# An expert layer's second matrix split in full for the large experts, with the router's steps in another order

## The chip, the cores and the metric

The kernel runs on one NeuronCore of one Trainium2 chip. The metric is the device time of one execution in microseconds. An execution is also recorded by the hardware profiler, and all durations below come from that one record.

## The reference

One decoder layer over 1024 tokens of width 1024, in float32: a modulated RMSNorm, a projection to two groups of attention heads (one dilated, one differential), an output projection with a gated residual, and then the part that matters here, a second norm and a mixture of 32 experts, of which each token takes four:

```python
h2 = rms_norm(x, norm2_g) * (1.0 + scale2) + shift2
logits = h @ w_router + b_router
top_val, top_idx = lax.top_k(logits, TOP_K)          # 4 of 32
gates = jax.nn.softmax(top_val, axis=-1)
...
def expert_block(args):
    xe, e = args
    gu = xe @ w_gate_up[e] + b_gate_up[e]            # 1024 -> 2048
    g = jnp.minimum(gu[:, :D_FF], SWIGLU_LIMIT)
    u = jnp.clip(gu[:, D_FF:], -SWIGLU_LIMIT, SWIGLU_LIMIT)
    act = (u + 1.0) * (g * jax.nn.sigmoid(SWIGLU_ALPHA * g))
    return act @ w_down[e] + b_down[e]               # 1024 -> 1024
...
return x + gate2 * y                                 # y: gate-weighted sum over a token's experts
```

All weights are float32: 3 x 1024 x 1024 numbers, 12 MB per expert.

## The kernel before

Tokens lie in eight blocks of 128. After attention (to about 608 us) the **router stage** runs block by block (`Block`, the loop over `b`), then the **expert stage** (744 to 2139 us) takes the 32 experts one after the other. On TensorE, ScalarE, VectorE and SyncE the instructions run in the order in which the code is written; GpSimd's order is set by the scheduler.

**Router stage.** For a block, `turn` transposes the attention rows, `products(n, ks)` multiplies eight k-tiles of them by one half of the output matrix (three products per tile), and `add` (L885, L886) adds the residual and squares it. The loop works on three blocks at a time: products of block `b`; for `b-1` the second norm, the transposes of its residual rows (`turn_x1`, L901), `rows_out` (VectorE's L909, GpSimd's L910, then a store of the rows to `h2d`) and `logits` (products with the router, top four by L920 to L924); for `b-2` `places` (each token's place within its expert), `listed` (products L958 that make the list of the first expert's tokens) and `scattered` (VectorE's L971 to L977 work out slot numbers, then four indirect stores by GpSimd, L979, write token and gate into a table `tab`). `TA`, `TC` say after which of the eight k-tiles the steps of the other blocks come. After the last block VectorE sorts the experts by their number of tokens (`key`, `order`).

**Expert stage.** Experts are taken in an order fixed in sorted ranks, with room for a fixed number of tokens ("places") per rank, large and small in turn: 172, 136, 200, 128, 136, 128, 188, 128, 140, 124, ..., 144, 120, 168, 116, 144, ..., 156, 96, so 17 of the 32 have 136 places or more. "Place 16" below is the one with 144 places at 1465 to 1506 us, place 17 the 120 behind it. Rows are gathered from `h2d` by GpSimd (L1144, `stage_g`), transposed on TensorE (L1172, `stage_t`) and split there into a high part, a remainder and a bf16 copy.

A weight matrix comes in chunks of 512 x 512 (1 MB, 12 per expert, numbered 0 to 11). A **split** chunk goes in two halves: ScalarE copies the high part (L826, `hb`), VectorE subtracts it from the chunk and stores the remainder as bf16 (L813, `ha`). `products` multiplies by it: 32 instructions L1194 (high weights by high part and remainder of the rows, side by side) and 32 instructions L1200 (remainder weights by the bf16 rows) for a quarter of a matrix. A **plain** chunk (numbers 8 and 9, the first half of `w_down`) is not split: L1250 takes it from its buffer `draw` at full precision. `pump(upto)` issues chunk loads while a buffer is free (`NRING` = 6 for split chunks, `NPL` = 2 for plain ones) and splits as long as no more than `NH` = 12 halves are ahead. `done` is called at 14 events in each expert, and the table `TG` says how many halves may have been split by each of them (`NSP` = 20 per expert).

An expert runs through four `products` calls for gate and up columns. After each, ScalarE evacuates one part of the sums with the bias (L1214, `tb`) and VectorE joins it with the other (L1216, L1218), with sigmoid (L1226, L1227), clamp (L1235) and product (L1236), into `a`. Then the plain half: for each of its two chunks 32 products L1250, in whose middle `a` is split for later (ScalarE's copy L1254, VectorE's L1255, GpSimd's cast L1256), and behind which the next expert's rows are transposed (`between`). ScalarE evacuates the four sums of the plain half (L1262) into `yT`, a tile of the buffer `ay` that also holds `a`. Then the split half (`products` with `ax`, `ab`), its four evacuations L1270 on ScalarE and the joins L1271 on VectorE. The result is transposed back (L1279) one event later, scaled by the gate and added to the output by an indirect store (L1180).

## Time and profile before

| | us |
|---|---|
| three runs | 2153.43, 2152.49, 2149.2 |
| median | 2152.49 |
| the profiled execution | 2153.28 |
| its span | 2151.5 |
| attention and before | to about 608 |
| router stage, start of the experts | 608 to 744 |
| expert stage | 744 to 2139 |

Engines are named PE (TensorE products), PEld (its weight loads), DVE (VectorE), ACT (ScalarE), POOL (GpSimd) and SP (SyncE, which issues the weight loads); L1194 is line 1194 of the kernel. A profile row tells how long an engine worked; whether that matters is told by the chain of work that ended last and by what an engine waited for.

### The profile page before, as it was taken

The page shows a single profiled execution, that of the slowest core. Times are in us where ns is not written, and L with a number is a line of the kernel's source. Part 1 is how long each engine was busy: PE and PEld are TensorE (multiplying, and loading weights), DVE is VectorE, ACT ScalarE, POOL GpSimd, SP SyncE. Part 2 cuts the span into 40 slices and gives each one's busy share as a digit, 9 for nine tenths or more (in the row PEclk, how much of TensorE's full clock was granted, in tenths as well). Part 3 has the DMA queues.
Part 4 walks back from the last instruction along what each step waited for, and adds up shares of the span by engine and source line. Part 5 has one row for each costly group of instructions (what it writes and reads, how often), then busy time and mean ns, then how long its engine had stood idle before and what let it go on. Part 6 is the DMA issues. An engine that isn't in the chain of part 4 may idle for free.

```text
span 2151.5 us, 43844 instructions
## 1 busy us (share of the span) xinstructions
PE 2042.9 (95%) x16922; PEld 1913.2 (89%) x16922; DVE 1643.5 (76%) x2831; ACT 1355.7 (63%) x2391; POOL 503.5 (23%) x473
## 2 busy tenths in 40 slices
PE   6999999999899599999999999999999999999997
PEld 5877778998777599999999999999999999999997
DVE  6587765777666778788788878888788878878884
ACT  3522314777633377677677677676777777768774
POOL 2255532112045411112111121111111211221211
PEclk9999999999999799999999999999999999999998
DMA  8267786442324599799899999999999999999993
GB/s 294 67 167 221 216 240 166 112 106 71 107 99 147 181 329 306 255 331 342 273 295 353 288 316 312 333 308 323 320 309 310 358 309 325 326 328 327 325 324 99
DMA packets 273654, 549.53 MB, mean 255 GB/s; under 512 B 31795, under 2 KB 31811, under 8 KB 273315
## 3 DMA queue, kind: packets, MB, share of 16 engines
q1 hardware_dynamic: 251507, 490.61, 67.7%
q0 software_dynamic: 21936, 56.09, 11.2%
q8 instruction: 134, 2.20, 0.4%
q14 instruction: 77, 0.63, 0.1%
HBM read 501.84 MB, written 44.78 MB: 254 GB/s over the span
## 4 chain that ended last, share of the span: by engine, by line
PE 45%; DVE 13%; ACT 9%; issue 6%; DMA 2%; POOL 0%; SPq 0%; ACTq 0%; POOLq 0%; DVEq 0%
PE gu L1194 25%; PE gu L1200 11%; PE gu L1250 5%; DVE ha L813 5%; ACT hb L826 4%; PE gu L1279 2%; PE po L605 1%; ACT ay L1262 1%; DMA eraw<-in_w_gate_up_dram 1%; DMA eraw<-in_w_down_dram 1%; DVE ax L1255 1%; ACT tb L1214 1%; DVE su L1235 1%; DVE su L1216 1%; DVE ixf L924 1%
## 5 line engine op out<-in xcount | busy, mean ns | idle before, releaser
L813 DVE TENSOR_TENSOR ha<-eraw,hb 128x1024 bf16<-128x1024 f32 x640 | 762.8, 1245 | 1.6 <-ACT hb L826 1.6
L826 ACT ACTIVATE hb<-eraw 128x1024 fp32r<-128x1024 f32 x640 | 634.2, 1051 | 13.4 <-DMA eraw<-in_w_down_dram 11.1
L1194 PE MATMUL gu<-xx,hb 128*128 128x256 f32 (+13 forms) x4096 | 587.7, 300 | 3.6 <-DVE xx L1176 3.6
L1194 PEld LDWEIGHTS gu<-xx,hb 128*128 128x128 f32 x4096 | 554.2, 190 | 4.5 <-DVE xx L1176 4.3
L1200 PEld LDWEIGHTS <-ha 128*128 128x128 bf16 x5120 | 310.8, 97 | 11.9 <-issue 1.5
L1200 PE MATMUL gu<-xb,ha 128*128 128x128 bf16 (+19 forms) x4096 | 271.6, 224 | 0.0
L1250 PE MATMUL gu<-ay,draw 128*128 128x128 f32 (+19 forms) x2048 | 267.6, 289 | 1.7 <-DVE ay L1236 1.7
L1250 PEld LDWEIGHTS gu<-ay,draw 128*128 128x128 f32 x2048 | 257.3, 191 | 2.7 <-DVE ay L1236 2.1
L1214 ACT ACTIVATE tb<-gu,bcol 128x128 f32<-128x128 f32 (+19 forms) x512 | 157.7, 370 | 97.2 <-PE gu L1200 85.5
L1194 PE MATMUL gu<-ax,hb 128*128 128x256 f32 (+13 forms) x1024 | 159.1, 314 | 26.1 <-ACT ay L1262 25.7
L1180 POOL DMA_INDIRECT out_dram<-y,slot x47 | 81.1, 1726 | 404.6 <-ACT y L1280 258.2
L1194 PEld LDWEIGHTS gu<-ax,hb 128*128 128x128 f32 x1024 | 148.5, 203 | 30.0 <-ACT ay L1262 28.8
L1144 POOL DMA_INDIRECT xg<-h2d,slot x47 | 70.3, 1496 | 352.9 <-PE gu L1172 89.2
L571 DVE CUSTOM_DVE_ANT_0 p<-pss,bias 128x1024 f32<-128x1024 f32 (+7 forms) x128 | 94.4, 755 | 49.7 <-ACT p L580 22.7
L1256 POOL CAST ab<-ax 128x512 bf16<-128x512 f32 (+19 forms) x64 | 68.4, 1072 | 266.8 <-ACT ax L1254 266.8
L1270 ACT ACTIVATE tb<-gu,bcol,g2c 128x128 f32<-128x128 f32 (+19 forms) x128 | 56.4, 466 | 107.7 <-PE gu L1200 77.9
L1271 DVE SCALAR_TENSOR_TENSOR ay<-gu,g2c,tb 128x128 f32<-128x128 f32 (+19 forms) x128 | 46.3, 362 | 96.3 <-ACT tb L1270 96.3
L605 PE MATMUL po<-vsb,pT 128*128 128x64 f32 (+1 forms) x864 | 109.6, 272 | 3.1 <-DVE kap L587 1.2
L1262 ACT ACTIVATE ay<-gu,bcol,g2c 128x128 f32<-128x128 f32 (+19 forms) x128 | 49.4, 466 | 99.9 <-DVE ax L1255 57.1
L605 PEld LDWEIGHTS po<-vsb,pT 128*128 128x128 f32 x864 | 103.9, 192 | 5.9 <-ACT pT L599 2.1
L580 ACT ACTIVATE p<-p,mn 128x1024 f32<-128x1024 f32 (+7 forms) x128 | 98.6, 773 | 13.8 <-DVE mn L571 13.0
L112 POOL TENSOR_TENSOR rrs<-vrs,nhalf 128x8 f32<-128x8 f32 (+2 forms) x48 | 66.6, 1387 | 171.8 <-DVE vrs L110 166.7
(274 smaller groups left out, 3120.8 us busy)
## 6 DMA issues: line engine op xcount, KB each, us to landing
eraw<-in_w_gate_up_dram SPq DMA_DIRECT2D x256, 1024.0 KB
draw<-in_w_down_dram SPq DMA_DIRECT2D x64, 1024.0 KB
eraw<-in_w_down_dram SPq DMA_DIRECT2D x64, 1024.0 KB
wraw<-in_w_ada_dram SPq DMA_DIRECT2D x32, 512.0 KB
wraw<-in_w_in_dram SPq DMA_DIRECT2D x23, 512.0 KB
hb<-in_w_ada_dram SPq DMA_DIRECT2D x16, 512.0 KB
qd<-tt POOLq DMA_DIRECT2D x32, 256.0 KB, 4.0
kd<-tt POOLq DMA_DIRECT2D x32, 256.0 KB, 4.7
```

Source lines behind the costliest of these rows:

```text
L571: nc.vector.tensor_tensor_reduce(p[:, :n], pss[:, :n], bias[:, (NB - 1 - ib) * P:(NB - 1 - ib) * P + n], -1.0, 3.0e38, OP.add, OP.min, mn)
L580: nc.scalar.activation(p, p, AF.Exp, bias=self.mn[c], scale=-1.0, accum_out=self.l[:, c:c + 1])
L605: nc.tensor.matmul(self.po[:, :w], self.pT[:, k], vsb[self.br][:, k, self.h * w:(self.h + 1) * w], start=(k == 0), stop=(k == self.ib))
L813: nc.vector.tensor_tensor(parts[t][1], raws[c][:, 2 * q:2 * q + 2], parts[t][0].bitcast(F32), OP.subtract)
L826: nc.scalar.activation(h_, raws[c][:, 2 * q:2 * q + 2], AF.Copy)
L1144: nc.gpsimd.indirect_dma_start(out=xg[:n], out_offset=None, in_=h2d, in_offset=bass.IndirectOffsetOnAxis(ap=sl.bitcast(I32)[:n, 0:1], axis=0))
L1180: nc.gpsimd.indirect_dma_start(out=out, out_offset=bass.IndirectOffsetOnAxis(ap=sl.bitcast(I32)[:n, 0:1], axis=0), in_=y[:n], in_offset=No ...
L1194: nc.tensor.matmul(pg[j // 2][:, j % 2, :max(256, 2 * C)], w[k][0][:, j * P:(j + 1) * P], xk[k], start=(k == 0), stop=False)
L1200: nc.tensor.matmul(pg[j // 2][:, j % 2, C:2 * C], w[k][1][:, j * P:(j + 1) * P], xb[:, k], start=False, stop=(k == KT - 1))
L1214: nc.scalar.activation(t[:, j], p[:, j, C:2 * C], AF.Identity, bias=bc[:, f + j:f + j + 1], scale=1.0)
L1250: nc.tensor.matmul(place(j), raw[:, k, j * P:(j + 1) * P], a[:, 4 * kh + k], start=(kh + k + j % 2 == 0), stop=(kh == 1 and k == 3 and j % ...
L1262: nc.scalar.activation(yT[:, j], place(j), AF.Identity, bias=bc[:, 2 * KT + j:2 * KT + j + 1], scale=g2c[:, j:j + 1])
```

## The change

Three parts are changed.

**Whole experts.** For the 17 experts with `CWH` = 136 places or more both halves of `w_down` are split, so all 12 chunks use the six common buffers, 24 halves are split per expert and the table of events is `TGW` (12 events). `activations(half)` splits each half of `a` as soon as it is made, and the first `products` call on `w_down` has the next expert's transposes in its middle (`mid`): high products of four k-tiles, low products of these, the transposes, then the rest. The sums of both halves leave through `outgoing`, the first half into a tile `yl` of its own.

**The other experts.** `plain` does what the plain half did, but its sums go to `yl` too, two of them after the second piece and two after the fourth.

**Router.** The residual rows are multiplied by the modulation before the norm's factor is known (`rows_start`, on VectorE) and finished by one VectorE instruction in `rows_out`. `scattered` is cut into `counted` (slot numbers) and `scattered` (the four stores). `listed`, `counted` and `scattered` of block `b-2` come behind `products(1, 0..1)`; the last block's stores come behind the gathers of the first expert; some tiles move to another pool, the splits before the expert loop are issued at two points only, and `overflow` (VectorE arithmetic on token counts) moves into the loop at the third expert.

```diff
-TA = 3
+TA = 4
 PB = 4
-TC = 5
+TC = 6
...
-SPL = dict(enumerate((0, 0, 0, 0, 0, 2, 4)))
+CWH = 136
+TGW = (12, 14, 16, 18, 19, 21, 23, 24, 26, 30, 31, 36)
...
+            whole = [CAPS[r] >= CWH for r in seq]
+            splits = [(i * NCH + c, q) for i in range(E) for c in range(NCH) if whole[i] or c not in PLAIN for q in range(2)]
+            base = [0]
+            for i in range(E):
+                base.append(base[-1] + (2 * NCH if whole[i] else 2 * (NCH - len(PLAIN))))
...
-                return "p" if d % NCH in PLAIN else "s"
+                return "p" if d % NCH in PLAIN and not whole[d // NCH] else "s"
...
+                def rows_start(self):
+                    self.h2 = ro.tile([P, D], F32, name="h2", bufs=1)
+                    nc.vector.tensor_mul(self.h2, self.x1, modb[:, 2])
                 def rows_out(self):
-                    h2 = ro.tile([P, D], F32, name="h2", bufs=1)
-                    nc.vector.scalar_tensor_tensor(h2, self.x1, self.r2, modb[:, 2], op0=OP.mult, op1=OP.mult)
-                    (nc.gpsimd if self.b < NB - 1 else nc.vector).tensor_tensor(h2, h2, modb[:, 1], OP.add)
-                    nc.sync.dma_start(h2d[self.rows, :], h2)
+                    nc.vector.scalar_tensor_tensor(self.h2, self.h2, self.r2, modb[:, 1], op0=OP.mult, op1=OP.add)
+                    nc.sync.dma_start(h2d[self.rows, :], self.h2)
...
-                def scattered(self):
-                    pay = self.pay
+                def counted(self):
                     pos = sm.tile([P, E], F32, name="pos")
                     nc.vector.tensor_add(pos, self.pp[:, :E], ebase)
                     nc.vector.tensor_mul(self.sel, self.sel, pos[:, None, :].to_broadcast([P, TOPK, E]))
                     slf = sm.tile([P, TOPK], F32, name="slf")
                     nc.vector.tensor_reduce(slf, self.sel, axis=AX.X, op=OP.add)
-                    sli = sm.tile([P, TOPK], I32, name="sli")
-                    nc.vector.tensor_copy(sli, slf)
+                    self.sli = (sm if self.b < NB - 1 else rt).tile([P, TOPK], I32, name="sli")
+                    nc.vector.tensor_copy(self.sli, slf)
                     nc.vector.tensor_add(mcum, mcum, self.msk)
+                def scattered(self):
...
-                    blocks[b - 2].scattered()
...
+                    pv.rows_start()
                     pv.rows_out()
                 norm_end(b + 1)
-                cur.products(0, range(TC, 6))
+                cur.products(0, range(TC, 7))
                 if nx:
                     nx.turn(0)
-                cur.products(0, range(6, 8))
-                if b > 1:
-                    blocks[b - 2].listed()
+                cur.products(0, range(7, 8))
                 if b == 0:
                     for g in range(2, 4):
                         split_wo(1, g)
                 cur.add(0)
                 cur.products(1, range(0, 2))
+                if b > 1:
+                    blocks[b - 2].listed()
+                    blocks[b - 2].counted()
+                    blocks[b - 2].scattered()
...
             pv.listed()
+            pv.counted()
             pv.scattered()
             cur.turn_x1(1)
-            pump(SPL[1])
-            pump(SPL[2])
+            cur.rows_start()
             cur.norm2()
             cur.logits()
             cur.rows_out()
-            pump(SPL[3])
             cur.places()
-            pump(SPL[4])
             cur.listed()
-            pump(SPL[5])
-            cur.scattered()
-            pump(SPL[6])
+            pump(2)
+            cur.counted()
+            pump(4)
...
+            tg = TGW if whole[i] else TG
+            pump(base[i] + tg[q])
+            event[:] = (i, q + 1) if q + 1 < len(tg) else (i + 1, 0)
...
-        def products(C, x, t0):
+        def products(C, x, t0, mid=None):
...
+            def low_products(js, ks):
+                for j in js:
+                    for k in ks:
+                        nc.tensor.matmul(pg[j // 2][:, j % 2, C:2 * C], w[k][1][:, j * P:(j + 1) * P], xb[:, k],
+                                         start=False, stop=(k == KT - 1))
...
+                    if mid:
+                        low_products(range(4), range(4))
+                        mid()
+            low_products(range(4), range(4 if mid else 0, KT))
             return pg
+        def plain(C, a, bc, d0, activations, between):
+            pg = banks()
+            def place(j):
+                return pg[:, j // 2, j % 2 * 256:j % 2 * 256 + C]
+            for kh in range(2):
+                raw = raws.pop(d0 + kh)
+                for j in range(4):
+                    for k in range(4):
+                        nc.tensor.matmul(place(j), raw[:, k, j * P:(j + 1) * P], a[:, 4 * kh + k],
+                                         start=(kh + k + j % 2 == 0), stop=(kh == 1 and k == 3 and j % 2 == 1))
+                    if j == 1:
+                        activations(kh)
+                    if kh and j % 2:
+                        if j == 1:
+                            yl = ap_.tile([P, 4, C], F32, name="yl")
+                        for f in (j - 1, j):
+                            nc.scalar.activation(yl[:, f], place(f), AF.Identity,
+                                                 bias=bc[:, 2 * KT + f:2 * KT + f + 1], scale=g2c[:, f:f + 1])
+                    if j == 1:
+                        done()
+                freed["p"] += 1
+                done()
+                between(kh)
+            return yl
...
+            def activations(kh):
+                f = slice(4 * kh, 4 * kh + 4)
+                nc.scalar.activation(ah[:, f, :C], a[:, f], AF.Copy)
+                nc.vector.tensor_sub(ah[:, f, C:], a[:, f], ah[:, f, :C].bitcast(F32))
+                nc.gpsimd.tensor_copy(ab[:, f], ah[:, f, :C].bitcast(F32))
...
+                if whole[i]:
+                    activations(half)
...
-                    if j == 1:
-                        f = slice(4 * kh, 4 * kh + 4)
-                        nc.scalar.activation(ah[:, f, :C], a[:, f], AF.Copy)
-                        nc.vector.tensor_sub(ah[:, f, C:], a[:, f], ah[:, f, :C].bitcast(F32))
-                        nc.gpsimd.tensor_copy(ab[:, f], ah[:, f, :C].bitcast(F32))
-                        done()
-                freed["p"] += 1
-                if kh:
-                    yT = ap_.tile([P, KT, C], F32, name="ay")
-                    for j in range(4):
-                        nc.scalar.activation(yT[:, j], place(j), AF.Identity,
-                                             bias=bc[:, 2 * KT + j:2 * KT + j + 1], scale=g2c[:, j:j + 1])
-                done()
-                between(kh)
...
+            if whole[i]:
+                pg = products(C, s_a, t0 + 16, lambda: between(0))
+                yl = ap_.tile([P, 4, C], F32, name="yl")
+                outgoing(yl, pg, 0)
+                done(high=2, low=4)
+                between(1)
+            else:
+                yl = plain(C, a, bc, d0, activations, between)
+            pg = products(C, s_a, t0 + (20 if whole[i] else 16))
+            yh = ap_.tile([P, KT, C], F32, name="ay")
+            outgoing(yh, pg, 4)
             done(high=2, low=4)
+            ys = [yl[:, f] for f in range(4)] + [yh[:, f] for f in range(4)]
...
         st = stage_g(0)
+        cur.scattered()
         stage_t(st, 0)
         stage_t(st, 1)
         lists(1)
-        pump(TG[-1] - NSP)
+        pump(12)
         mans.close()
-        tot = overflow()
         order_s.enter_context(tc.manual_schedule(engines={mybir.EngineType.PE, mybir.EngineType.Activation,
                                                           mybir.EngineType.DVE, mybir.EngineType.SP}))
         for i in range(E):
+            if i == 2:
+                tot = overflow()
```

On ScalarE, in place 17 (120 places, a plain one) from the last evacuation of the up columns (`tb<-gu,bcol`) to the copy of the next expert's rows (`xx<-gu`), the order before was:

```order
L1214 ACTIVATE tb<-gu,bcol 128x120 x4
L826 ACTIVATE hb<-eraw 128x1024
L1254 ACTIVATE ax<-ay 128x4x120
L826 ACTIVATE hb<-eraw 128x1024 x3
L1254 ACTIVATE ax<-ay 128x4x120
L826 ACTIVATE hb<-eraw 128x1024
L1262 ACTIVATE ay<-gu,bcol,g2c 128x120 x4
L826 ACTIVATE hb<-eraw 128x1024
L1175 ACTIVATE xx<-gu 128x8x128
```

and is now:

```order
L1264 ACTIVATE tb<-gu,bcol 128x120 x4
L828 ACTIVATE hb<-eraw 128x1024
L1255 ACTIVATE ax<-ay 128x4x120
L828 ACTIVATE hb<-eraw 128x1024 x3
L1255 ACTIVATE ax<-ay 128x4x120
L1236 ACTIVATE yl<-gu,bcol,g2c 128x120 x2
L828 ACTIVATE hb<-eraw_18527 128x1024
L1236 ACTIVATE yl<-gu,bcol,g2c 128x120 x2
L828 ACTIVATE hb<-eraw_18527 128x1024
L1180 ACTIVATE xx<-gu 128x8x128
```

The four evacuations of the plain half are cut in two pairs with a split between them, and write `yl` where they wrote the buffer of `a`.

On VectorE, in place 16 (144 places, a whole one now), from the last product that makes `a` (`ay<-gt,su`), the order before was:

```order
L1236 SCALAR_TENSOR_TENSOR ay<-gt,su 128x288
L813 TENSOR_TENSOR ha<-eraw,hb 128x1024
L1255 TENSOR_TENSOR ax<-ay,ax 128x4x144
L813 TENSOR_TENSOR ha<-eraw,hb 128x1024 x3
L1165 TENSOR_TENSOR bcol<-bcol,g2c 128x8
L1255 TENSOR_TENSOR ax<-ay,ax 128x4x144
L813 TENSOR_TENSOR ha<-eraw,hb 128x1024
L813 TENSOR_TENSOR ha<-eraw_17363,hb 128x1024
L1176 TENSOR_TENSOR xx<-gu,xx 128x8x120
L1271 SCALAR_TENSOR_TENSOR ay<-gu,g2c,tb 128x144 x4
```

and is now:

```order
L1286 SCALAR_TENSOR_TENSOR ay<-gt,su 128x288
L1256 TENSOR_TENSOR ax<-ay,ax 128x4x144
L815 TENSOR_TENSOR ha<-eraw,hb 128x1024 x3
L1170 TENSOR_TENSOR bcol<-bcol,g2c 128x8
L1297 SCALAR_TENSOR_TENSOR yl<-gu,g2c,tb 128x144 x4
L815 TENSOR_TENSOR ha<-eraw,hb 128x1024
L815 TENSOR_TENSOR ha<-eraw_17877,hb 128x1024 x2
L815 TENSOR_TENSOR ha<-eraw,hb 128x1024
L1181 TENSOR_TENSOR xx<-gu,xx 128x8x120
L815 TENSOR_TENSOR ha<-eraw,hb 128x1024
L1297 SCALAR_TENSOR_TENSOR ay<-gu,g2c,tb 128x144 x4
```

The second split of `a` now follows directly on `a`, and four joins and more subtractions of weights stand between it and the joins of the second half.

On GpSimd, at the start of the expert stage (the last step of a norm, the last block's table stores, the gathers of the first expert), the order before was:

```order
L112 TENSOR_TENSOR rr_7415<-vr_7413,nhalf 128x1
L979 DMA tab<-pay,sli 36864x2 x4
L1144 DMA xg<-h2d,slots_2972 128x1024
L979 DMA tab<-pay,sli 36864x2 x4
L1144 DMA xg<-h2d,slots_2973 44x1024
```

and is now:

```order
L113 TENSOR_TENSOR rr_7418<-vr_7416,nhalf 128x1
L984 DMA tab<-pay,sli 36864x2 x4
L1149 DMA xg<-h2d,slots_2975 128x1024
L1149 DMA xg<-h2d,slots_2976 44x1024
L984 DMA tab<-pay,sli 36864x2 x4
```

The last block's four stores stand behind both gathers.

## Rows read from the trace of the kernel before

**Rows 1.** The page: busy time of each engine, and DMA busy tenths by slice.

```profile
PE 2042.9 (95%) x16922; PEld 1913.2 (89%) x16922; DVE 1643.5 (76%) x2831; ACT 1355.7 (63%) x2391; POOL 503.5 (23%) x473
...
DMA  8267786442324599799899999999999999999993
```

**Rows 2.** Chain that ended last, places 16 and 17: start us, us, what.

```profile
1491.32 3.97 PE gu L1250 x32
...
1500.04 4.27 PE gu L1194 x32
1504.31 2.02 PE gu L1200 x32
...
1519.15 2.91 PE gu L1194 x24
```

**Rows 3.** The chain in place 2, with 200 places.

```profile
874.86 5.44 PE gu L1250 x32
...
886.59 5.82 PE gu L1194 x32
892.40 2.76 PE gu L1200 x32
```

**Rows 4.** TensorE's waits, 744 to 2150 us: us in total, times, longest us.

```profile
PE gu L1194 <- ACT ay L1262: 25.7, 15, 1.8
```

**Rows 5.** Timeline of place 17: start us, us, instruction, [idle before <-releaser].

```profile
1539.15 1.23 PE L1194 MATMUL gu<-ax,hb 128*128 128x256 f32 x8
...
1539.92 0.65 DVE L1255 TENSOR_TENSOR ax<-ay,ax 128x480 fp32r<-128x480 f32 x1
1540.49 2.35 DVE L813 TENSOR_TENSOR ha<-eraw,hb 128x1024 bf16<-128x1024 f32 x2
1540.66 1.48 ACT L1262 ACTIVATE ay<-gu,bcol,g2c 128x120 f32<-128x120 f32 x4 [3.20 <-DVE ax L1255]
...
1542.20 4.63 PE L1194 MATMUL gu<-ax,hb 128*128 128x256 f32 x24 [1.82 <-ACT ay L1262]
```

**Rows 6.** Windows of places 2, 16, 17, the stage: PE, PEld, DVE, ACT, POOL, clock, DMA.

```profile
838.32:894.94 56.62, 56.62 (x412) 55.49 (x410) 38.93 (x47) 34.74 (x52) 10.39 (x7) 1.00 0.81 273
...
1465.02:1506.13 41.11, 41.11 (x404) 40.72 (x402) 35.71 (x47) 31.61 (x50) 6.46 (x8) 1.00 0.95 332
1506.13:1548.34 42.21, 40.39 (x421) 39.37 (x418) 34.32 (x48) 31.80 (x52) 8.07 (x7) 0.96 1.00 329
...
744.00:2100.00 1356.00, 1326.46 (x12638) 1302.26 (x12639) 1104.00 (x1450) 994.53 (x1582) 255.09 (x226) 0.99 0.96 317
```

**Rows 7.** Groups in place 16: count | busy us, mean ns | idle before, releaser.

```profile
L813 DVE TENSOR_TENSOR ha<-eraw,hb 128x1024 bf16<-128x1024 f32 x20 | 24.2, 1264 | 0.0
...
L1271 DVE SCALAR_TENSOR_TENSOR ay<-gu,g2c,tb 128x120 f32<-128x120 f32 (+1 forms) x5 | 1.7, 348 | 4.3 <-ACT tb L1270 4.3
...
L1227 DVE TENSOR_TENSOR gt<-gt,su 128x576 f32<-128x576 f32 x2 | 1.5, 759 | 1.5 <-ACT su L1226 1.5
L1254 ACT ACTIVATE ax<-ay 128x576 fp32r<-128x576 f32 x2 | 1.4, 678 | 0.0
```

**Rows 8.** TensorE's waits in the router stage, 608 to 714 us.

```profile
PE p L958 <- DVE pos L971: 5.0, 6, 0.9
PE pt L901 <- DVE osb L886: 3.0, 5, 0.6
```

**Rows 9.** Timeline of the router stage and of the experts' start.

```profile
643.34 2.58 DVE L924 CAST ixf<-ix 128x4 f32<-128x4 uint32 x1
...
643.47 2.41 POOL L910 TENSOR_TENSOR h<-h,modb 128x1024 f32<-128x1024 f32 x1
...
720.82 0.17 DVE L924 CAST ixf<-ix 128x4 f32<-128x4 uint32 x1
...
727.80 1.51 POOL L1144 DMA_INDIRECT xg<-h2d,slots  x1 [2.73 <-DVE slots L963]
...
735.57 0.97 POOL L1144 DMA_INDIRECT xg<-h2d,slots  x1 [0.30 <-issue]
```

## What the change should do: the prediction

> **What bounds the kernel now.** I read the page first [rows 1]: TensorE is busy for 95% of the span, and the DMA line stands at 7 to 9 in the expert stage (744 to 2139 us, the 15th of the 40 slices on), so the weights are the second thing to watch. The window over that stage [rows 6] has TensorE busy for 1326 of 1356 us: the stage must be shortened on TensorE. Then the chain inside two experts: one with 144 places [rows 2] and one with 200 [rows 3]. There the TensorE pieces join without a gap, so these experts go at TensorE's pace, and a half of the second matrix is one kind of piece or the other: full-precision products straight from the loaded chunk (L1250), or split products (L1194 and L1200). The waits of the stage come third [rows 4]: one entry is large, the last split half (L1194) waiting for the ScalarE instructions L1262, 15 times. The timeline of one such place [rows 5] shows the reason: eight products start at 1539.15, the ninth needs the bank that the plain half's sums still fill, and the four L1262 run from 1540.66. They had been waiting for VectorE's L1255, because their output shares a buffer with `a`, which L1255 still reads. Last, the windows of single experts [rows 6], for VectorE's load and the granted clock, and its groups within one expert [rows 7], with one of ScalarE's.
>
> **The split half in place of the plain one.** At 144 places the first plain piece takes 3.97 and the second the like, 7.94 together; the split half takes 4.27 (L1194) plus 2.02 (L1200), 6.29 [rows 2]. That saves 1.65 us. At 200 places it is 2 x 5.44 = 10.88 against 5.82 + 2.76 = 8.58, or 2.30 [rows 3]. The 17 experts concerned (16 large ones and the first in the order, 172) have 2700 places, 159 on the mean; between the two points that is 1.83 each, 31 us in all, all on TensorE's path.
>
> **The wait for L1262.** Eight products took 3.05 us from start to the ninth's start, where 24 at full clock take 2.91 [rows 2], 0.97 for eight; 2.1 are lost. The view has 25.7 us of idle time for 15 waits [rows 4], about 1.9 each with the pipeline's own gap: 28 us. Behind some of these waits TensorE runs at the lower of its two levels: the 24 products took 4.63 [rows 5] instead of 2.91, and the window of that expert has a granted clock of 0.96 [rows 6]. Seven of the experts' windows read 0.96, this one among them. Seven times 1.7 is 12 us. In the changed order of ScalarE two of the four evacuations stand before a split and all four write `yl`, which nobody else holds. The transposes and eight products lie between the plain half and the ninth product; the four evacuations together take 1.48 [rows 5], two of them already beside the plain half. So both amounts go, 40 us. After that the split of `a` (L1255, ended at 1540.57) is next, needed by the 17th product, 1.94 after 1539.15. That leaves half a microsecond, so VectorE is late next.
>
> **What VectorE gets to do.** Each large expert adds four subtractions (L813; two in a row take 2.35 [rows 5], and 20 take 24.2 [rows 7], so I take 1.15 each) and four joins (L1271, 0.35 each [rows 7]): 4.6 + 1.4 = 6.0 us, 102 us over 17. ScalarE gets four copies (1.0 each) on 31.61 of 41.11 [rows 6] and keeps its eight evacuations, so it stays under TensorE's time. VectorE's 6.0 does not always. Take the pair of places 16 and 17, 144 and 120 places [rows 6]: VectorE is busy for 35.71 + 34.32, so 76.0 with the addition. To this come waits which its fixed order can't fill: for ScalarE's sigmoid, 1.5 per expert [rows 7], 3.0; for the copy of `a` (L1254), which now directly precedes the subtraction, its 0.7 and the hand-over, twice, 1.6 [rows 7]; about 1 of the kind that L1271 already has for L1270 (4.3 [rows 7]). That is 81.6. TensorE would need 83.3 - 1.65 - 3.6 = 78.1. So this pair gives back 3.5 of its 5.2. At 200 places VectorE has 38.93 of 56.62 [rows 6]: 56.62 - 2.30 - 38.93 - 6.0 leaves it 9.4, as much as these waits and the overflow arithmetic (about 5, moved there) take with some left, and nothing is given back. Nine of the large experts have 156 places or fewer; 9 x 3.5, and half a microsecond for each of the other eight, is 36 us. Bounds: if the twelve split pieces that are held ahead level this out, only the short waits remain that the new order itself brings. TensorE wants the second half of `a` split after 16 split products, 16 low ones and the transposes, some 3.5 us at 144 places (half of 6.29, and the transposes), and joins, copy and subtraction take about as long: half a microsecond per large expert as an estimate, 8 us in 17. If nothing levels it out, the full 102 us come back. I take 36, since the pair's rows are nearest.
>
> The Trainium skill ("SBUF — State Buffer", section "Who interferes with whom") says that a VectorE instruction with two SBUF inputs and a GpSimd instruction that reads SBUF lock each other out. It would make each added subtraction dearer where it meets a cast on GpSimd. As an estimate by that rule, one hit of half a microsecond per large expert would be 8 us more. The mean of 1.264 [rows 7] against 1.15 a piece in a row shows that the existing subtractions pay some of this already, so I add nothing.
>
> **The router stage.** Two TensorE waits stand in it: 5.0 us for the list products (L958) and 3.0 for the turn of the residual rows (L901) [rows 8]. The second follows from VectorE's L924, 2.58 us while GpSimd's L910 runs and 0.17 without it [rows 9]. The change takes L910 from GpSimd and gives VectorE a product of two 128 x 1024 operands (1.2 us, as L813 [rows 7]) in its place, so VectorE wins some 1.2 per block; and it puts one more group of products ahead of the turn and four ahead of the list products. The table scatters and their slot products move behind the lists, past nothing on VectorE that TensorE waits for. I take all 8.0.
>
> **The start of the experts.** The last block's scatters stood between the two gathers of expert 0 on GpSimd: 727.80 and 735.57 [rows 9]. Behind the change the second gather follows the first after its 1.51 and a pause of 0.3, near 729.6, 5.9 earlier; the first gather itself starts about as now, since the new product ahead of the norm costs what the sum behind it saves. The scatters run during expert 0's staging and the rows that wait for the table are those of expert 1, needed 40 us later. So 6 us; the lower bound is 3 if VectorE's key sorting then ends last, the upper 8.
>
> **Sum.** -31 - 40 + 36 - 8 - 6 = -49. The profiled execution took 2153.3 (span 2151.5), so 2104; the median of the runs is 0.8 below it: 2103 us.
>
> **Rivals.** (a) The pieces held ahead level VectorE's load: 36 becomes 8, 2075 us. For it: in the large experts VectorE has idle time now (5.4 of 41.1 [rows 6]). Against: the small ones have little once TensorE's wait goes. (b) The weights end last. The stage moves 317 GB/s at a DMA share of 0.96 [rows 6], and 35 us saved in it asks for 325. If 322 were all, 21 us could be saved there: 2153.3 - 21 - 14 - 0.8 = 2118. For it: the large experts' four added chunks use the six common buffers and leave the two others idle. Against it: the expert at 1465.02 had 332 GB/s for 41 us, and TensorE never waited [rows 6]. The Trainium skill (the same page, section "A bandwidth-pool intuition that's wrong") gives about 358 GB/s as one core's share of the HBM; as an estimate by that page the limit would allow 155 us less in the stage, and (b) would not happen; none of the rows here reaches that figure. (c) Slower: VectorE's added work comes whole onto TensorE's path in every large expert, because the subtractions stand ahead of the joins that free the product banks. That is 102 back instead of 36: 2169. It turns slower than now from 85/17 = 5.0 us per large expert; the rows bear 3.5 at worst. (d) The bank is still not free: ScalarE is late through its splits, the 40 us stay and the wait hides part of VectorE's lag, 36 becomes 10: 2116.
>
> **Chances.** Forecast (2088 to 2112) 0.50; (a) 0.20; (b) 0.15; (c) 0.05; (d) 0.10. About 0.2% (4.3 us) is what a measurement can tell from no change. The range reaches to (a) and (b) with some room, 2074 to 2130, and leaves out (c) and the tails. Faster 0.91, same 0.04, slower 0.05.
>
> **What would show it.** In the profile after: TensorE's pieces of the large experts' second matrix as split products only; the entry for the evacuation wait gone and the windows at 0.96 fewer; TensorE idle before products whose release is VectorE, most at 136 to 156 places; L924 at 0.17 throughout; the two gathers next to each other and the first expert product near 738. DMA releases ahead of ScalarE's splits, more than a few, would mean (b). The prediction is wrong in its main step if the pairs of 136 to 156 places shrink by more than 4 us, or not at all.

## The result: slower by 2.5%

The changed kernel takes 2206.86 us (median of four runs, 2203.1 to 2209.26), the kernel before 2152.96 beside it. The ratio is 1.0251 with an interval of 1.0234 to 1.0267: 54 us slower, where 49 us faster was forecast and 2074 to 2130 was the range.

TensorE's waits from 720 to 2200 us in the changed kernel (us in total, times, longest) answer to [rows 4]:

```profile
PE gu L1207 <- DVE ax L1256: 33.7, 16, 2.9
PE gu L1207 <- DVE xx L1181: 15.8, 15, 2.2
PE gu L1228 <- ACT yl L1236: 15.5, 15, 1.2
PE gu L1319 <- DVE ay L1297: 9.3, 33, 0.5
PE gu L1207 <- ACT y L1320: 8.4, 16, 0.8
```

The former entry of 25.7 us is gone, and five others stand in its place. The largest is the split of `a` on VectorE, once in nearly every whole expert. The windows of places 2, 16 and 17 answer to [rows 6], in the same columns:

```profile
847.49:904.69 57.20, 54.65 (x409) 52.99 (x409) 49.76 (x107) 37.96 (x55) 11.17 (x7) 1.00 0.73 243
1485.46:1531.82 46.36, 41.82 (x405) 40.49 (x402) 39.08 (x53) 34.33 (x53) 8.20 (x8) 0.96 0.82 274
1531.82:1573.48 41.66, 39.54 (x416) 37.97 (x417) 36.55 (x50) 32.66 (x53) 8.48 (x7) 1.00 1.03 355
```

Place 16 went from 41.11 to 46.36 us. The granted clock of 0.96 has moved from the plain place 17 to the whole place 16: of the 31 windows between first products, those of the ten places 136 to 160 read 0.93 to 0.96 now and 1.00 before, and no small one is below 1.00, where seven were. VectorE is busy 39.08 + 36.55 = 75.6 us in the pair, as forecast (76.0), but the pair lasts 88.0, where it took 83.3 before and 81.6 were forecast. The timeline of place 16 where its second half of `a` is made:

```profile
1510.06 4.62 DVE L815 TENSOR_TENSOR ha<-eraw,hb 128x1024 bf16<-128x1024 f32 x4
...
1513.70 1.18 PE L1201 MATMUL gu<-ab,ha 128*128 128x144 bf16 x16
1514.60 0.45 DVE L1266 SCALAR_TENSOR_TENSOR su<-tb,gu 128x288 f32<-128x288 f32 x1
...
1517.12 0.68 ACT L1255 ACTIVATE ax<-ay 128x576 fp32r<-128x576 f32 x1 [2.89 <-DVE ay L1286]
...
1517.84 0.76 DVE L1256 TENSOR_TENSOR ax<-ay,ax 128x576 fp32r<-128x576 f32 x1 [0.75 <-ACT ax L1255]
...
1518.65 3.84 PE L1207 MATMUL gu<-ax,hb 128*128 128x288 f32 x16 [2.91 <-DVE ax L1256]
```

VectorE works through four subtractions before it reaches the joins at 1514.60, and `a` is split 2.91 us after TensorE wants it. The 16 products behind that wait take 3.84 us, where the 16 ahead of it took 2.33: TensorE runs at the lower of its two levels for a while, which is the window's 0.96. What VectorE itself waited for from 800 to 2150 us:

```profile
DVE ay L1297 <- ACT tb L1295: 49.6, 73, 1.4
DVE gt L1277 <- ACT su L1276: 44.2, 60, 0.9
DVE gt L1268 <- ACT tb L1264: 36.0, 43, 1.9
DVE yl L1297 <- ACT tb L1295: 30.4, 45, 1.7
DVE ax L1256 <- ACT ax L1255: 26.8, 32, 1.1
```

Together 187 us, all for ScalarE. In the chain that ended last VectorE's subtractions have 10% now (from the page; 5% before):

```profile
PE gu L1207 21%; DVE ha L815 10%; PE gu L1201 8%; ACT hb L828 6%; ACT tb L1295 1%; ACT ax L1255 1%; PE gu L1228 1%; PE po L606 1%; ACT tb L1264 1%; DVE su L1266 1%; DVE yl L1297 1%; DVE xx L1181 1%; DMA tab<-pay,sli 1%; ACT y L1320 1%; DVE ay L1297 1%
```

### The profile page after: what moved, and what is told of

It reads as the page before. It is cut to its first block, busy times and chain, and to the rows that moved or that the text cites. A ratio compares the mean times of both kernels' runs of the same rounds, so it can differ in the third digit from the quotient of the medians.

```text
span 2206.7 us, 44091 instructions
## 1 busy us (share of the span) xinstructions
PE 2048.3 (93%) x16922; PEld 1899.3 (86%) x16922; DVE 1731.8 (78%) x2974; ACT 1419.0 (64%) x2459; POOL 490.6 (22%) x466
## 3 DMA queue, kind: packets, MB, share of 16 engines
q1 hardware_dynamic: 251507, 490.61, 64.8%
## 4 chain that ended last, share of the span: by engine, by line
PE 37%; DVE 18%; ACT 13%; issue 6%; DMA 2%; POOL 1%; ACTq 0%; POOLq 0%; DVEq 0%; SPq 0%
PE gu L1207 21%; DVE ha L815 10%; PE gu L1201 8%; ACT hb L828 6%; ACT tb L1295 1%; ACT ax L1255 1%; PE gu L1228 1%; PE po L606 1%; ACT tb L1264 1%; DVE su L1266 1%; DVE yl L1297 1%; DVE xx L1181 1%; DMA tab<-pay,sli 1%; ACT y L1320 1%; DVE ay L1297 1%
## 5 line engine op out<-in xcount | busy, mean ns | idle before, releaser
L815 DVE TENSOR_TENSOR ha<-eraw,hb 128x1024 bf16<-128x1024 f32 x708 | 844.7, 1248 | 0.0
L828 ACT ACTIVATE hb<-eraw 128x1024 fp32r<-128x1024 f32 x708 | 695.2, 1048 | 1.6 <-DMA eraw<-in_w_down_dram 1.6
L1207 PE MATMUL gu<-ax,hb 128*128 128x256 f32 (+13 forms) x1568 | 249.6, 317 | 35.0 <-DVE ax L1256 33.7
L1207 PEld LDWEIGHTS gu<-ax,hb 128*128 128x128 f32 x1568 | 231.4, 200 | 41.6 <-DVE ax L1256 37.0
L1295 ACT ACTIVATE tb<-gu,bcol,g2c 128x172 f32<-128x172 f32 (+19 forms) x196 | 87.3, 470 | 142.0 <-PE gu L1201 81.0
L1228 PE MATMUL gu<-ay,draw 128*128 128x128 f32 (+6 forms) x960 | 117.8, 279 | 15.5 <-ACT yl L1236 15.5
L1228 PEld LDWEIGHTS gu<-ay,draw 128*128 128x128 f32 x960 | 110.5, 192 | 18.8 <-ACT yl L1236 18.2
L1201 PE MATMUL gu<-ab,ha 128*128 128x136 bf16 (+19 forms) x1568 | 112.9, 228 | 0.0
L113 POOL TENSOR_TENSOR rrs<-vrs,nhalf 128x8 f32<-128x8 f32 (+2 forms) x48 | 66.2, 1379 | 170.3 <-DVE vrs L111 168.5
L1255 ACT ACTIVATE ax<-ay 128x512 fp32r<-128x512 f32 (+19 forms) x64 | 42.8, 669 | 93.0 <-DVE ay L1286 93.0
L460 PE MATMUL pp<-wh,hb 128*128 128x512 f32 x240 | 100.1, 417 | 0.0
```

The lines of the kernel that those rows point to most:

```text
L460: nc.tensor.matmul(pp, hh[b][:, k], wh[:, kk], start=(k == 0), stop=False)
L815: nc.vector.tensor_tensor(parts[t][1], raws[c][:, 2 * q:2 * q + 2], parts[t][0].bitcast(F32), OP.subtract)
L828: nc.scalar.activation(h_, raws[c][:, 2 * q:2 * q + 2], AF.Copy)
L1201: nc.tensor.matmul(pg[j // 2][:, j % 2, C:2 * C], w[k][1][:, j * P:(j + 1) * P], xb[:, k], start=False, stop=(k == KT - 1))
L1207: nc.tensor.matmul(pg[j // 2][:, j % 2, :max(256, 2 * C)], w[k][0][:, j * P:(j + 1) * P], xk[k], start=(k == 0), stop=False)
L1228: nc.tensor.matmul(place(j), raw[:, k, j * P:(j + 1) * P], a[:, 4 * kh + k], start=(kh + k + j % 2 == 0), stop=(kh == 1 and k == 3 and j % ...
```

## The experiments

Each time stands beside runs of the kernel before on the same chip, whose medians are 2151.6 to 2153.4 us. Runs of one letter share a chip; those of different letters compare to within some 2 us. "Places 136 to 160" (10 experts), "164 and more" (7) and "small" (14) are sums of the times between the first products of successive experts, in the profiled run:

| kernel | us | 136 to 160 | 164 and more | small |
|---|---|---|---|---|
| before | 2152.96 | 423.8 | 354.0 | 578.4 |
| changed | 2206.86 | 470.3 | 352.3 | 582.8 |
| a1: no whole experts | 2153.14 | 434.1 | 362.3 | 556.0 |
| a3: old plain half | 2240.15 | 467.9 | 354.4 | 618.0 |
| b4: a1 with late sums | 2119.42 | 428.0 | 354.1 | 540.0 |
| c4: changed, late sums | 2199.53 | 469.9 | 355.8 | 575.9 |
| d1: c4, joins in pairs | 2154.26 | 455.7 | 348.0 | 549.8 |
| d2: b4, seven buffers, joins in pairs | 2109.90 | 423.1 | 354.5 | 541.2 |

**The parts, undone one at a time.** First no expert is whole (a1):

```diff
-CWH = 136
+CWH = 999
```

> The changed kernel with no expert treated as whole (the bound is set to 999 places), the rest of the change kept. Theory 1 (VectorE: the four added subtractions and four joins per large expert stand on the path of TensorE's products): the large experts return to their former durations, 45 us, and their small neighbours lose what VectorE hands on to them, some 5 to 10 us more: 2150 to 2160 us. Theory 2 (the plain half's sums, evacuated in two pairs, hold up the remaining plain products, and all experts pay for it): the 17 large experts, plain again, pay that wait too, so 2165 to 2185 us. By the prediction's own sum, in which the split half was worth 31 us and VectorE gave 36 back, 2202 us.

It took 2153.14 us: the whole experts cost 54, as much as the whole loss. Theory 1 gave the time, but not alone: the large experts are 18.6 us above those of before, because the plain half's new evacuation makes TensorE wait in every expert. Its wait, and one place of it in the timeline:

```profile
PE gu L1228 <- ACT yl L1236: 30.9, 32, 2.0
```

```profile
1536.97 2.04 PE L1228 MATMUL gu<-ay,draw 128*128 128x120 f32 x16
1539.90 2.04 PE L1228 MATMUL gu<-ay,draw 128*128 128x120 f32 x16 [0.88 <-ACT yl L1236]
```

The second 16 products of a chunk wait for the evacuation of the first pair of sums, about 1 us in each of 32 experts. The small ones gain 22.4 us all the same.

Then the router part alone is undone (a2: the loop of the blocks, `rows_out`, the stores and `overflow` as before; the tiles stay in their pools).

> The changed kernel with the router stage, the start of the experts and the place of the overflow arithmetic as before. The first expert product came at 747.3 us in the changed kernel and at 744.4 before, so theory 1 (the reordered router is worth nothing or costs a little): 2200 to 2207 us, first expert product near 744, third expert 3 to 5 us shorter. Rival (the reordered router does what the prediction said, and the profiled run hides it): 2215 to 2222 us.

2204.09 us, not told from the changed kernel's 2206.86: the reordered router gained nothing here. The first expert product stayed late (747.5), and the third expert was 2.8 us shorter.

Third, the plain half with its four sums in the buffer of `a` again (a3):

```diff
-                        for f in (j - 1, j):
-                            nc.scalar.activation(yl[:, f], place(f), ...)
...
+                if kh:
+                    yl = ap_.tile([P, KT, C], F32, name="ay")
+                    for f in range(4):
+                        nc.scalar.activation(yl[:, f], place(f), ...)
```

> The changed kernel with the plain half as before: its four sums evacuated behind the last plain product into the buffer that also holds the activation. The prediction put 40 us on this step. Theory 1 (in the 15 small experts TensorE is held up elsewhere for as long, by VectorE and by the evacuation between the plain products): the wait of about 1.8 us and the stretch at the lower clock come back where 3.5 us of other waits go, 2200 to 2212 us. Rival (the step is worth what was predicted): 2235 to 2250 us.

2240.15 us, the rival. The old wait comes back, 30.9 us in 14 times, and with its lower clock it costs the small experts 35 us. So the step is worth 33 us beside whole experts, near what was predicted.

Last, only the eight largest are whole (a4, `CWH = 160`):

> The changed kernel with experts of 160 places or more as whole ones (8) and the nine of 136 to 156 plain. Theory 1 (VectorE decides, and has room in the largest experts alone): the nine lose 43 us of added time and their neighbours some more, 2150 to 2163 us, and no slower than the kernel without whole experts by more than 2 us. Rival (the whole experts cost something that doesn't depend on their size, such as the shared loading buffers): the cost falls with their number, 8 of 17, so half of it stays, 2178 to 2185 us.

2162.02 us (1.0042, 1.0025 to 1.0059), 9 above a1. The time is within theory 1's range, but its condition of at most 2 us above a1 failed, so even these do not pay: those of 164 and more take 350.4 where a1 has 362.3, but the small ones go from 556.0 to 569.8, and 160 places lose too.

**VectorE's load or its order.** The load is added to the kernel before, with nothing else changed (b1):

```diff
-                nc.vector.tensor_tensor(parts[t][1], raws[c]..., OP.subtract)
+                for _ in range(2 if c % NCH in (10, 11) and CAPS[seq[c // NCH]] >= 136 else 1):
+                    nc.vector.tensor_tensor(parts[t][1], raws[c]..., OP.subtract)
```

> The kernel before, with four of VectorE's weight subtractions (those of chunks 10 and 11) issued twice in each of the 17 experts with 136 places or more. The second one writes the same values again; TensorE, ScalarE and the loads do the same work as before. Theory L (VectorE's load decides: what it does plus its waits for ScalarE fills the expert): 35.7 busy + 4.6 + 5.5 of waits against 41.1 us of TensorE at 144 places, some 4.7 us more in each of the nine experts of 136 to 156 places and little in the largest, 2190 to 2205 us. Theory O (the load is levelled out by the twelve pieces held ahead, and the changed kernel loses by the order in which the splits stand before the joins): 2153 to 2163 us.

2190.24 us, 38.6 more, with TensorE's work untouched; 136 to 160 places carry 29.7 of it, some 3 each where theory L had 4.7, and 4.6 stand ahead of the first expert product (749.1), where the added work does not reach. Place 16 takes 44.68 us instead of 41.11, with VectorE busy for 39.69 instead of 35.71:

```profile
1484.35:1529.03 44.68, 42.07 (x405) 40.82 (x402) 39.69 (x51) 31.48 (x50) 7.76 (x8) 1.00 0.91 296
```

Theory O's forecast that the pieces held ahead level the load out falls.

Then the load is taken from the changed kernel (b2):

```diff
+                if c % NCH in PLAIN:
+                    nc.vector.memset(parts[t][1], 0.0)
+                else:
-                nc.vector.tensor_tensor(parts[t][1], ...)
+                    nc.vector.tensor_tensor(parts[t][1], ...)
```

> The changed kernel with the four added subtractions of each whole expert (chunks 8 and 9) replaced by a VectorE instruction that only writes zeros into the remainder, so that half of the second matrix has no remainder part; everything else stays in its order. A write without operands should take less than half of the 1.15 us, so VectorE gets back some 3 us per whole expert. Theory L: the experts of 136 to 160 places shorten by 3 to 4.5 us each, 2160 to 2178 us. Theory O (the splits that stand directly ahead of the last joins of the activation, pieces 19 to 22 of the expert, cause the wait; only one of them is among the lightened ones): 2190 to 2205 us.

2177.8 us, 29.1 less, and places 136 to 160 are 30.3 shorter. Groups of VectorE in place 16, and the window of that place:

```profile
L818 DVE TENSOR_TENSOR ha<-eraw,hb 128x1024 bf16<-128x1024 f32 x19 | 23.1, 1268 | 0.1
L816 DVE MEMSET ha<- 128x512 uint32 x4 | 1.9, 485 | 0.2
```

```profile
1477.16:1520.50 43.34, 40.14 (x404) 39.00 (x401) 36.70 (x53) 34.33 (x53) 8.10 (x8) 1.00 0.87 293
```

Four times 1.27 - 0.49 is 3.1 us less work, and the place is 3.0 shorter. Not all of it is TensorE's waiting: 1.3 us are, and 1.7 are its busy time (41.82 to 40.14), as the granted clock is back at 1.00.

The order is changed with the same load (b3, the table of events):

```diff
-TGW = (12, 14, 16, 18, 19, 21, 23, 24, 26, 30, 31, 36)
+TGW = (12, 16, 16, 20, 20, 20, 20, 23, 27, 28, 32, 36)
```

> The changed kernel with another table of events for whole experts, (12, 16, 16, 20, 20, 20, 20, 23, 27, 28, 32, 36): the same 24 splits, none of them ahead of the joins that make the second half of the activation, and one instead of four ahead of the next expert's rows. Theory O: the wait of 2.9 us for the second split of the activation and the 1.7 us at the lower clock behind it go, 17 times at most, with the 1.4 us at the next expert's first product: 2130 to 2165 us. Theory L: the same work meets TensorE at another place, 2195 to 2215 us.

2227.91 us, outside both ranges: the wait for `a` is nearly gone (3.6 us), and VectorE is late at the joins instead:

```profile
PE gu L1207 <- DVE yl L1297: 74.2, 16, 5.8
```

The pair of places 16 and 17 takes 87.8 us, as in the changed kernel (88.0). That speaks for the load. But at the same load the order alone cost 21 us more than in the changed kernel: places of 164 and more went from 352.3 to 386.9, those of 136 to 160 from 470.3 to 481.5, and the small ones from 582.8 to 561.5. So the order decides too, above all where VectorE had time left.

**The plain half without its new wait.** The four sums are evacuated together behind the last plain product, into `yl` (b4, no whole experts):

```diff
-                    if kh and j % 2:
-                        ...
+                if kh:
+                    yl = ap_.tile([P, 4, C], F32, name="yl")
+                    for f in range(4):
+                        nc.scalar.activation(yl[:, f], place(f), ...)
```

> The changed kernel without whole experts (2153.1 us), and the plain half's four sums evacuated together behind its last product, still into their own tile. In that kernel TensorE waits 32 times, 30.9 us in all, for the first pair of these evacuations in the middle of the second plain chunk, because both pairs of sums lie in one PSUM tile. Theory: this wait goes whole, and neither the former wait for the evacuations (they no longer wait for VectorE) nor the lower clock behind it comes back: 2118 to 2126 us. Rival (the evacuations, late again, hold up the ninth product of the split half as before): 2140 to 2155 us.

2119.42 us (0.9849, 0.9832 to 0.9865). Places 16 and 17, for [rows 6]:

```profile
1446.28:1487.38 41.10, 41.10 (x405) 40.72 (x402) 35.50 (x47) 31.58 (x50) 7.12 (x8) 1.00 1.05 359
1487.38:1525.96 38.58, 38.58 (x420) 37.78 (x418) 34.23 (x48) 31.79 (x52) 9.01 (x7) 1.00 0.98 333
```

TensorE is never idle in them, and place 17 is 3.6 us shorter than before the change. Against a1, 33.7 us are regained where the trace of a1 had a wait of 30.9.

On this kernel the old router is tried again (c1):

> The kernel with the late sums and no whole experts (2119.4 us), with the router stage, the experts' start and the place of the overflow arithmetic as before. Theory (the reordered router gains nothing: it starts the experts some 5 us sooner after the last block, and loses as much in the blocks, where the norm waits on GpSimd): 2115 to 2123 us. Rival (it is worth the predicted 14 us): 2131 to 2135 us.

2122.26 us, 2.8 above b4, but on another chip: by the ratios to the kernel before (0.9853 and 0.9849) it is 1 us, not told from nothing. The rival falls. In the changed kernel GpSimd's timeline of the router stage shows:

```profile
688.40 0.96 POOL L984 DMA_INDIRECT tab<-pay,sli  x1 [0.30 <-issue]
692.77 0.14 POOL L946 IOTA pay<- 128x4 int32 x1 [3.41 <-DMA tab<-pay,sli]
692.87 0.57 POOL L113 TENSOR_TENSOR rr<-vr,nhalf 128x1 f32<-128x1 f32 x1
```

The fill of a later block's `pay` waits for the stores just issued, and the norm's L113 stands behind it. This comes four times, 11.7 us in all. With more buffers (c2):

```diff
-                    pay = (...).tile([P, TOPK, 2], F32, name="pay")
+                    pay = (...).tile([P, TOPK, 2], F32, name="pay", bufs=7 if self.b < NB - 1 else 1)
```

> The kernel with the late sums and no whole experts (2119.4 us), with seven buffers instead of three for the tile that holds tokens and gates for the table stores. In the changed kernel GpSimd waits 11.7 us in four places of the router stage: it fills this tile for a later block directly behind the stores of the block that holds the buffer, and the norm's power instruction, which TensorE needs, stands behind it. Theory: the four waits go, and the blocks of the router stage become 1 to 2 us shorter, 2112 to 2117 us. Rival (the norm is not on the path): 2117 to 2122 us.

2113.02 us, 6.4 less (8.6 by the ratios); the wait is gone. From the first product of the router stage to the last block's first it is 108.6 us. With three buffers it was 116.3 in b4 and 116.3 to 122.1 in all ten such runs, and 115.2 to 115.5 in the four with the old router.

**Whole experts on top of that.** Five of them (c3, `CWH = 172`), and all 17 (c4):

> The kernel with the late sums (2119.4 us), with the five experts of 172 places and more as whole ones. Theory: TensorE saves 1.7 us in each of the four last of them, where VectorE has room, and the small expert behind each loses 2 to 3 us, because the five splits at the last event stand ahead of its first steps; the one with 200 places carries the overflow arithmetic too: 2119 to 2127 us. Rival (where VectorE has room the split half is a plain gain): 2109 to 2113 us.

> The changed kernel with all 17 whole experts, and the late sums in the other 15. Theory (in a kernel with whole experts VectorE sets the time of the small neighbours too, so that they can't use what the late sums give): 2190 to 2200 us, 70 to 80 us above the same kernel without whole experts. Rival (the small experts gain as they did without whole ones, 3 us each): 2155 to 2165 us.

2127.38 us, just above the theory's range, and 2199.53, within it; both rivals fall. In c3 the place of 188 gains 1.77 us, and the 128 behind it loses 2.56. In c4 the whole experts cost 80 us: 41.9 in places 136 to 160, 35.9 in the small ones.

**VectorE's waits.** Open was whether its waits for ScalarE cost as its work does. The outgoing sums go two at a time (d1 on c4, d2 on c2). The edit also uses both halves of `tb`, so that all four sums of a half fit into its two buffers; what the order and what this room gives was not separated:

```diff
-                for j in range(4):
-                    t = ap_.tile([P, 2, C], F32, name="tb", bufs=2)[:, 0]
-                    nc.scalar.activation(t, ...)
-                    nc.vector.scalar_tensor_tensor(dst[:, j], ...)
+                for q in range(2):
+                    t = ap_.tile([P, 2, C], F32, name="tb", bufs=2)
+                    for j in range(2 * q, 2 * q + 2):
+                        nc.scalar.activation(t[:, j % 2], ...)
+                    for j in range(2 * q, 2 * q + 2):
+                        nc.vector.scalar_tensor_tensor(dst[:, j], ...)
```

> The kernel with 17 whole experts and the late sums (2199.5 us), with the outgoing sums evacuated and joined two at a time instead of one at a time: ScalarE evacuates both sums of a bank pair before VectorE joins them, with the same number and size of instructions. One at a time, the joins wait 65.6 us for these evacuations over the stage, some 0.5 us each for two of four. Theory (VectorE's waits for ScalarE, which its fixed order doesn't fill, stand on the path in whole experts and their neighbours just as its work does): about 0.6 us less for each of 49 outgoing halves, so 20 to 30 us, 2170 to 2180 us. Rival (such a wait is slack: work held ahead fills it): 2194 to 2202 us.

> The kernel without whole experts, with the late sums and the seven buffers (2113.0 us), with the same joins in pairs. Theory: TensorE sets the time of nearly all experts here, so VectorE's waits cost nothing and their loss gains little: 2106 to 2114 us, nearly all of it in the four experts of 140 and 144 places that have waits for VectorE. Rival (the waits count here too): 2085 to 2100 us.

d1 took 2154.26 us, 45 less, well above the 20 to 30 expected. VectorE's waits for these evacuations in c4, then in d1:

```profile
DVE ay L1296 <- ACT tb L1294: 33.6, 63, 0.6
DVE yl L1296 <- ACT tb L1294: 32.0, 44, 2.0
```

```profile
DVE yl L1297 <- ACT tb L1294: 13.0, 17, 2.0
DVE ay L1297 <- ACT tb L1294: 9.2, 18, 1.2
```

65.6 us became 22.2: 43 us of waits went, and 45 us of time. That the two agree so well is in part luck, for some of the 45 came through the clock: ten of the 31 windows read below 1.00 in c4 and seven in d1. 26 of it came in the small experts. The windows of places 16 and 17, in c4 and in d1:

```profile
1481.84:1528.06 46.22, 41.76 (x401) 40.56 (x401) 39.01 (x53) 34.33 (x53) 8.20 (x8) 0.96 0.84 279
1528.06:1569.39 41.33, 39.55 (x416) 37.98 (x416) 37.38 (x50) 32.66 (x53) 8.65 (x7) 1.00 1.02 353
```

```profile
1459.10:1503.28 44.18, 40.19 (x401) 39.06 (x401) 38.53 (x53) 33.65 (x53) 8.47 (x8) 1.00 0.91 299
1503.28:1543.60 40.32, 39.18 (x417) 37.95 (x417) 37.38 (x50) 33.10 (x55) 10.20 (x7) 1.00 1.05 363
```

Even so d1 is 35 us above b4: TensorE's wait for the split of `a` stays (33.1 us, 34.3 in c4).

d2 took 2109.90 us (0.9802, 0.9785 to 0.9818), 3.1 less than c2 and, by the ratios, 1.5, with overlapping intervals. VectorE's waits for these evacuations went from 79.0 to 64.8 us, and at most 3 us of time with them: where TensorE sets the pace such waits are mostly slack. d2 is faster than the kernel before and the changed one.

## Why the prediction was wrong

The miss is 104 us, and a1 divides it. The whole experts cost 54 us where the sum had 5 (-31 + 36), 49 of the miss. The rest of the change, which was to gain 54 (40 + 8 + 6), gained nothing in a1.

**The split half** was read rightly in direction, and somewhat too high: with 188 places the changed kernel's expert is 1.79 us shorter, where the line between the prediction's two points gives 2.2.

**What VectorE gets to do** is the step that failed. The work was right (76.0 forecast for the pair, 75.6 measured). The waits that its fixed order can't fill were put at 5.6 us and are 88.0 - 75.6 = 12.4 (13.0 by the rows, which overlap a little). VectorE's waits in the pair, from 1485.46 to 1573.48 us of the changed kernel:

```profile
DVE ay L1297 <- ACT tb L1295: 4.6, 6, 1.4
DVE gt L1277 <- ACT su L1276: 2.8, 4, 0.8
DVE yl L1297 <- ACT tb L1295: 2.1, 3, 1.1
DVE gt L1268 <- ACT tb L1264: 1.9, 3, 1.2
DVE ax L1256 <- ACT ax L1255: 1.6, 2, 0.8
```

The terms for the sigmoid (3.0) and for the copy of `a` (1.6) came true. The term for the joins, "about 1", is 6.7, and the 1.9 of L1268 were not in the sum. The row was at hand: the joins' 4.3 us behind L1270 in one expert [rows 7], of which I counted 1, taking the rest for slack that added work would use up. d1 shows that they are not slack: where VectorE is the bound, taking them away shortens the kernel. So this pair gave back 9.9 us (88.0 over the 78.1 that TensorE would need) instead of 3.5, and all together an estimated 111 instead of 36 between b4 and c4 (the 80 lost, and the forecast 31). Rival (c) had nearly this price, 102, and 0.05; it placed it in the large experts alone. Of the 80, 36 are in the small experts behind them, and in the seven largest saving and loss nearly cancel (355.8 us for 354.1). Why the small neighbours pay was not separated in full. In c4 VectorE is busy for 37.38 us in place 17 against 34.23 in b4, with 50 instructions against 48. But in the changed kernel's place 17 the chain spends more on ScalarE's splits (L828, 22%) than on VectorE's (L815, 8%), five of them in a row (4.56 us): ScalarE's queue is a rival there that no run isolates.

Two readings beside it were off, and nothing hangs on them. The gap between 1.264 and 1.15 us of a subtraction is mostly the overlap of records: one is recorded with 1.218 (median), and in a row they start 1.14 apart. In the changed kernel the median is 1.217, so contention did not make them dearer. And the terms of rival (d) add up to 2118, not 2116.

**The wait for L1262** went with its clock, as forecast. The step's own new wait was missed: `yl` is evacuated between plain products, and the products behind it wait. I costed that edit by who else holds `yl` and never asked who else uses the sums' tile. The wait took 31 us over 32 experts in a1, as much as the step gave; late sums with the old router (c1) give 31 of the predicted 40. In the small experts they give 38 (578.4 to 540.0); places 136 to 160 lose some 4 again.

**The router stage.** L924's 2.58 us are gone (0.17 in all eight blocks), and with c2's buffers the blocks take 6.8 us less than with the old router, near the predicted 8. With the buffers of the change the gain is lost, and in the changed kernel the blocks take 4.0 us more (119.2 against 115.2): on GpSimd, past whose queue I had moved the stores without naming what stands behind them.

**The start** came nearly true in the changed kernel: from the last block's first product to the first expert product it is 42.0 us, 47.1 before (44.4 in b4), so 5 of the forecast 6. The two gathers stand next to each other (732.76 and 734.30), but in the chain the second lands 8.38 us after its start where it took 4.26; what made it longer was not tried. The first expert product still came at 747.3 and not near 738, behind the longer blocks and a router stage that began 3.8 us later (its first product stands at 582.2 before, ahead of the 608 given for the end of attention, and at 586.0 now).

**The weights**, rival (b), did not end last in the changed kernel: ScalarE's splits wait for them once, 1.6 us. In the faster kernels they begin to count. From 760 to 2050 us ScalarE waits for them in b4:

```profile
ACT hb L828 <- DMA eraw<-in_w_down_dram: 35.2, 14, 7.3
ACT hb L828 <- DMA eraw<-in_w_gate_up_dram: 1.5, 4, 0.9
```

Before, it was 13.3 us there. In b4's place 12 (140 places, 1.8 us longer than before) one weight load has half of the chain. The Trainium skill ("SBUF — State Buffer", section "A bandwidth-pool intuition that's wrong") gives about 358 GB/s as one core's share of the HBM. The trace of b4 has that figure in place 16 (359), with TensorE never waiting, and the changed kernel's small experts go up to 364, a little above it; no run here shows the limit itself.

## What to carry to other kernels

Before work is moved to an engine with idle time, ask of each idle stretch what ended it: a wait for another engine in a fixed order is not room, and it adds to the load as soon as that engine becomes the bound. Compare load plus such waits, not load, with the bound. When a result is read earlier from a tile that is still being written, look for the writer's next instruction; when DMAs are issued later, look for what waits for their buffers in the issuing queue.

## What the runs showed of the hardware

The stage ahead of the router, which the change leaves as it was, ended 1.4 to 4.6 us later in the other profiled runs (first router product at 583.6 to 586.8 us, 582.2 before), b1 among them, which has the old code there; so the change alone does not explain it. In the changed kernel the stretch of 530 to 586 us has a granted clock of 0.94, where 530 to 582 before has 1.00.

TensorE's lower clock came behind some of its waits, and moved with them. Before, seven windows of small experts read 0.96, with 15 waits of up to 1.8 us; in the changed kernel place 16, with a wait of 2.9 us, reads 0.96, and the small experts read 1.00. The 32 waits of about 1 us in a1 (up to 2.0) left every window but the first at 1.00.

A VectorE write of 128 x 1024 bf16 zeros took 0.485 us against 1.27 for the subtraction that writes the same tile.
